# A macaron encoder layer on one core: unnormalised rows in the first gate products, 1/rms applied where they are resumed, twelve products begun ahead, norm weights loaded as rows

## The chip, the core and the metric

The kernel runs on one core of a Trainium2 chip. The metric is device microseconds of one execution; lower is better. Engines are named as the profile names them: PE (TensorE matmuls) with PEld (its weight loads), DVE (VectorE), ACT (ScalarE), POOL (GpSimd) and SP (SyncE, which issues most DMAs here; SPq is its queue).

## The reference, cut to what matters

```
x = x + 0.5 * swiglu(rms_norm(x, ffn1_norm), w_gate, w_up, w_down)     # first feed-forward
h = rms_norm(x, mix_norm); ... attention and mLSTM share one projection; x = x + merged @ w_out
x = x + 0.5 * swiglu(rms_norm(x, ffn2_norm), ...)                      # second feed-forward
return rms_norm(x, final_norm)

rms_norm(x, g) = x * rsqrt(mean(x*x) + eps) * g
swiglu(x, wg, wu, wd) = (silu(x @ wg) * (x @ wu)) @ wd
```

There are two sequences (`x_prompt`, `x_sample`) of 512 tokens with 1024 features; the feed-forwards have 2816 hidden features. All is float32. `rms_norm` multiplies each token (row of x) by one number, 1/rms, so `(x * g) @ w` can be taken first and each token's result multiplied by its 1/rms afterwards.

## The kernel before

**Precision.** A float32 operand is split into a high part (an ACT copy to fp32r, the format that TensorE multiplies) and a low part (DVE: source minus high). `product` (line 327) makes one 128x128 by 128x512 product of half the contraction: for each of four k it issues three matmuls (high·high, high·low, low·high), so 12 matmuls.

**Both sequences at once.** The 22 blocks (`NF`) of 128 hidden features are computed for both sequences together as a two-by-two block product with seven sub-products instead of eight (Strassen's scheme with Winograd's sums). The sums of operands are made by `right_sums` (line 281, for x) and `gu_left_b` (for weights). The seven operands are named `B11, B21, B22, T1, T2_, T3, T4`; two of them, `B11` and `B21`, hold only sequence 0 and only gate weights. Their product, `B11` plus `B21` in one PSUM bank, is the gate pre-activation of sequence 0.

**Begun ahead.** Because `B11` and `B21` need sequence 0 alone, `Up.begin` (line 438) computes them for the first `AHEAD` = 10 blocks while sequence 1 is still being loaded, turned, normed and summed: 24 matmuls each. The two results, `v1` (after `B11`) and `g0` (Silu of the whole), go to DRAM (`kept`). `Up.rest` then runs through all blocks in the order `ORDER`: a "resumed" block loads its pair (`resume`, two loads) and does five products, 60 matmuls; a "fresh" block does all seven, 84. Resumed and fresh alternate for eight pairs, then come four fresh and two resumed. In `gu_rest` (line 350) a fresh block's products are taken in the order B11, T2, B21, T1, T3, B22, T4, a resumed one's T2, T1, T3, B22, T4:

```
V_.tensor_tensor(u2, v1, Y, op=ALU.add)      # L364: needs v1 and product T2 in bank Y
product(Z, W[T1], xc[T1], True)
...
product(Y, W[T3], xc[T3], False)             # adds into the bank that L364 has read
```

So T3's first matmul waits for L364. `Sides.out` splits the results again and stores them (`rbuf`, a ring of seven SBUF rows, `ring.rows["o"]`) for the down projection.

**The start.** `load_x(0)` loads x_prompt in four blocks of 128 tokens; a first weight load, pinned behind the second block, and x_sample follow. As each block arrives, DVE and ACT sum its squares (`rows_rstd`, lines 1268 and 1270). PE turns the eight 128-feature groups (four 128x128 transposes each, L1251), ACT copies them out (`keep_x`, L1256), a chain of twelve small DVE operations makes 1/rms (`rsqrt_cols`, lines 162 to 192), four PE transposes broadcast it (L213), DVE multiplies every group by gain and 1/rms (L1275), and ACT and DVE split it (`put`, L278 and L279). Only then is a matmul of block 0 possible. The norm weights are loaded with the access `"(k p) -> p k"`, which takes one element at a time: 1024 elements of 4 bytes for `g1`, `gm` and `g2`, 512 for `hn`.

**Order.** A scheduler places instructions within each engine by priority; `pin` (`keep_in_program_order`) fixes a written order, `shifted(n)` changes a priority. Each engine and each DMA queue runs its list strictly in order.

## Time and profile before

| | |
|---|---|
| median of 3 runs | 2078.68 us (2077.52 to 2079.41) |
| the profiled execution: its time, its span | 2079.39 us, 2077.5 us |
| mean granted TensorE clock | 0.998 |
| busy: PE, PEld, DVE, ACT, POOL | 99%, 81%, 74%, 43%, 5% of the span |
| first products begun (B11, B21) until the first resumed block | 18.2 to 79.2 us |
| `Up.rest` of the first feed-forward | 79.2 to 446.9 us |

A row of the timeline gives start, duration (of the whole group where "xN" follows), engine, source line, operation, output<-input, shapes, and in brackets how long the engine had been idle and what ended that. Rows of one engine overlap by a few hundredths of a us, so the step between starts, not the duration, is what one instruction costs in a run of many. In a table of stretches each engine has its busy us and, in brackets, its instruction count; then come the granted TensorE clock, the DMA engines' busy share and GB/s.

### The profile page before, as it was taken

To read this page: it belongs to the slowest core of one execution; us is meant where nothing else is said; L and a number is where in the kernel's file an instruction comes from. 1 tells how busy PE (TensorE), PEld (TensorE's weight loads), DVE (VectorE), ACT (ScalarE), POOL (GpSimd) and SP (SyncE) were. 2 spreads that over 40 slices of the span, in tenths; PEclk is the share of its full clock that TensorE was granted. 3 is DMA by queue.
4 is the path that set the end of the run, shared out by engine and by line. 5 is a ranking of instruction groups with operands and counts; after the bars stand their busy time and mean duration, and the time that the engine had idled before them with its cause. 6 is when DMAs were issued, how large, how long until landed. Compare 5 with 4: busy or idle time off the path is not lost.

```text
span 2077.5 us, 27122 instructions
## 1 busy us (share of the span) xinstructions
PE 2059.7 (99%) x9451; PEld 1689.1 (81%) x9451; DVE 1547.5 (74%) x2798; ACT 901.6 (43%) x1653; POOL 103.7 (5%) x118
## 2 busy tenths in 40 slices
PE   8999999999999999999999999999999999999998
PEld 6888888888888877888877788888888888888887
DVE  7888888786797897575567645545888888796697
ACT  6544444442234566463344443323544444443224
POOL 1000000001003000100120000002000000000001
PEclk9999999999999999999999999999999999999999
DMA  9656555699766654777675245677656555599753
GB/s 280 206 171 195 193 172 183 197 338 365 267 218 239 219 159 170 260 240 271 218 270 176 102 152 183 204 255 239 210 168 220 176 190 182 166 346 350 267 204 125
DMA packets 307064, 454.31 MB, mean 219 GB/s; under 512 B 20064, under 2 KB 178864, under 8 KB 305904
## 3 DMA queue, kind: packets, MB, share of 16 engines
q1 hardware_dynamic: 304912, 446.87, 64.0%
q0 software_dynamic: 1872, 5.46, 0.8%
q8 instruction: 74, 1.21, 0.2%
q14 instruction: 62, 0.51, 0.1%
q10 hardware_dynamic: 144, 0.26, 0.0%
HBM read 285.63 MB, written 166.89 MB: 218 GB/s over the span
## 4 chain that ended last, share of the span: by engine, by line
PE 94%; DVE 2%; DMA 1%; ACT 1%; issue 0%; SPq 0%; ACTq 0%; DVEq 0%
PE mm L770 20%; PE pss L333 17%; PE pst L333 11%; PE mm L333 10%; PE mm L589 8%; PE pst L589 4%; PE pss L589 4%; PE mm L754 4%; PE pso L589 3%; PE pso L1044 1%; PE pss L1017 1%; PE pso L754 1%; PE pst L1036 1%; PE pso L1180 1%; PE pst L770 1%; PE pss L770 1%
## 5 line engine op out<-in xcount | busy, mean ns | idle before, releaser
L770 PE MATMUL mm<-xh,w 128*128 128x512 f32 x896 | 290.4, 394 | 0.0
L333 PE MATMUL pss<-xc,w 128*128 128x512 f32 x1056 | 256.3, 391 | 0.4 <-DVE t L364 0.4
L333 PE MATMUL mm<-xc,w 128*128 128x512 f32 x1056 | 253.1, 390 | 2.0 <-ACT w L291 1.0
L333 PE MATMUL pst<-xc,w 128*128 128x512 f32 x1056 | 253.8, 389 | 0.0
L333 PEld LDWEIGHTS pss<-xc,w 128*128 128x128 f32 x1056 | 196.9, 188 | 47.6 <-DVE t L364 7.0
L333 PEld LDWEIGHTS mm<-xc,w 128*128 128x128 f32 x1056 | 197.4, 188 | 44.8 <-ACT w L291 1.9
L333 PEld LDWEIGHTS pst<-xc,w 128*128 128x128 f32 x1056 | 198.1, 188 | 41.5 <-ACT t L368 0.4
L770 PEld LDWEIGHTS mm<-xh,w 128*128 128x128 f32 x896 | 167.7, 188 | 33.6
L589 PE MATMUL mm<-rt,w 128*128 128x512 f32 x765 | 178.8, 389 | 0.0
L770 PE MATMUL mm<-xl,w 128*128 128x512 f32 x448 | 176.3, 394 | 0.0
L589 PEld LDWEIGHTS mm<-rt,w 128*128 128x128 f32 x765 | 143.5, 188 | 29.8
L291 ACT ACTIVATE w<-t 128x512 fp32r<-128x512 f32 x176 | 106.9, 627 | 139.0 <-issue 55.2
L292 DVE TENSOR_TENSOR w<-t,w 128x512 fp32r<-128x512 f32 x176 | 118.1, 688 | 55.7 <-ACT w L291 53.8
L333 PE MATMUL pss<-xc,f 128*128 128x512 f32 x528 | 126.8, 389 | 0.0
L333 PEld LDWEIGHTS pss<-xc,f 128*128 128x128 f32 x528 | 99.1, 188 | 20.6
L672 ACT ACTIVATE w<-wr 128x512 fp32r<-128x512 f32 x72 | 45.1, 632 | 138.5 <-PE pso L589 65.2
L672 ACT ACTIVATE w<-t 128x512 fp32r<-128x512 f32 x82 | 51.8, 632 | 107.4 <-PE pst L589 62.4
L770 PEld LDWEIGHTS mm<-xl,w 128*128 128x128 f32 x448 | 84.3, 188 | 16.6
L589 PE MATMUL pss<-rt,w 128*128 128x512 f32 x396 | 93.7, 389 | 0.0
L589 PE MATMUL pst<-rt,w 128*128 128x512 f32 x396 | 93.7, 389 | 0.0
L239 ACT ACTIVATE w<-wr 128x1024 fp32r<-128x1024 f32 (+1 forms) x56 | 57.2, 1027 | 74.0 <-PE mm L770 30.3
L589 PEld LDWEIGHTS pst<-rt,w 128*128 128x128 f32 x396 | 74.3, 188 | 15.4
(359 smaller groups left out, 3653.6 us busy)
## 6 DMA issues: line engine op xcount, KB each, us to landing
rt<-rbuf SPq DMA_DIRECT2D x154, 512.0 KB, 5.5
wpark<-w SPq DMA_DIRECT2D x104, 512.0 KB, 3.4
w<-wpark SPq DMA_DIRECT2D x104, 512.0 KB, 4.6
wr<-in_ffn_w_gate_dram SPq DMA_DIRECT2D x62, 512.0 KB, 5.3
rbuf<-tab SPq DMA_DIRECT2D x102, 256.0 KB, 4.0
wr<-in_ffn_w_up_dram SPq DMA_DIRECT2D x44, 512.0 KB, 4.6
rbuf<-f SPq DMA_DIRECT2D x72, 256.0 KB, 4.0
wr<-in_w_in_dram SPq DMA_DIRECT2D x36, 512.0 KB, 6.0
```

The costliest lines, as they stand in the source:

```text
L239: pin(nc.scalar.activation(hi, raw, AF.Copy))
L291: pin(nc.scalar.activation(t[:, 0], src, AF.Copy))
L292: pin(V_.tensor_tensor(t[:, 1], src, f(t[:, 0]), op=ALU.subtract))
L333: nc.tensor.matmul(p, a[:, k, :], xt[:, b, k, :], start=(first and k == 0 and i == 0), stop=(k == HK_ - 1 and i == 2), skip_group_check=True)
L589: nc.tensor.matmul(p, u[:, a, d * P:(d + 1) * P], r[:, b, ts], start=(first and q == 0 and k == 0), stop=(q == len(us) - 1 and k == 2), sk ...
L672: nc.scalar.activation(hi, src, AF.Copy)
L754: nc.tensor.matmul(p[b][:, :N], a[:, k, bs], w_[:, kl, :], start=(k == 0 and i == 0), stop=(k == KD - 1 and i == 2))
L770: nc.tensor.matmul(p, a[:, k, :], b, start=(k == 0 and i == 0), stop=(k == n - 1 and i == 2))
L1017: nc.tensor.matmul(p, qT[:, h, b * P:(b + 1) * P], kv[:, hk * 2 + j, :], start=(j == 0), stop=(j == 1))
L1036: nc.tensor.transpose(p[:, b * P:(b + 1) * P], Ps[b][:, kb * P:(kb + 1) * P], ident)
L1044: nc.tensor.matmul(po, Vst[:, kv_, hk, :], w, start=(kv_ == 0 and i == 0), stop=(kv_ == 3 and i == 1))
L1180: nc.tensor.matmul(po, vm[:, a, t, hs_], b, start=(t == 0 and n == 0), stop=(t == 3 and n == 2))
```

## The change

It has four parts.

1. The start. x_prompt's rows are turned and split without 1/rms: `first_x` takes each turned group from PSUM, ACT writes gain times x as the high part, DVE the rest as the low part. Six of the eight groups hold their banks while the four token blocks arrive, each block turned as it lands; two matmuls of ones (`busy(2)`) are placed between blocks. The first weight load stands directly behind x_prompt, in two halves, and is split in two halves too. 1/rms of sequence 0 is worked out after that and kept as a row table, `R0`. The float32 copies of x0 are multiplied by gain and `R0` later, in the loop that makes the sums.
2. Where they are resumed. `begin` stores the unscaled products (`Copy` in place of `Silu`). `scale_first` multiplies `v1` and `g0` by `R0` on POOL and applies Silu on ACT: for resumed blocks after their loads, for fresh blocks after the copies out of PSUM. `R0` takes one of the seven rows of ring "o" in the first feed-forward. In that feed-forward POOL gets 44 multiplications of 128x512, and ACT 22 more Silus.
3. `AHEAD` is 12, in both feed-forwards. `ORDER` becomes ten pairs of resumed and fresh and two resumed.
4. The four norm weights are loaded as 8 (or 4) rows of 128 elements and turned on PE; the load of the gate bias moves to the start.

In the changed program POOL's list in a pair reads: resumed block's `g0`, its `v1`, the fresh block's `v1`, its `g0`. DVE's list around the pair is otherwise as before (L364 is L378 there).

```diff
-    def gu_left_a(rg, pin=lambda i: i):
+    def gu_left_a(rg, lo=None, pin=None, between=None):
         wa = w8_tile()
-        w_pair(wa, rg.rearrange("p (a k) c -> p a k c", a=2), pin)
+        rv = rg.rearrange("p (a k) c -> p a k c", a=2)
+        if between:
+            for a in range(2):
+                w_pair(wa[:, :, a], rv[:, a], lo, pin)
+                between()
+        else:
+            w_pair(wa, rv, lo, pin or (lambda i: i))
...
+    def scale_first(row, v1, g0):
+        if v1 is not None:
+            G_.tensor_tensor(v1, v1, row, op=ALU.mult)
+        if g0 is not None:
+            G_.tensor_tensor(g0, g0, row, op=ALU.mult)
+            nc.scalar.activation(g0, g0, AF.Silu)
...
             X = gu_first_a(W, xc, v1)
+            if row is not None:
+                scale_first(row, v1, None)
             second()
-            gu_first_b(X, W, xc, g0)
+            gu_first_b(X, W, xc, g0, AF.Silu if row is None else AF.Copy)
+            if row is not None:
+                scale_first(row, None, g0)
...
-    AHEAD = 10
+    AHEAD = 12
...
             self.ring.rows["o"] += tables(FFN_ROWS)
+            if row:
+                self.row = self.ring.rows["o"].pop()
...
                 for t, d in zip(got, self.kept.pop(j)):
                     nc.sync.dma_start(t, d)
+                if self.row is not None:
+                    scale_first(self.row, *got)
...
+    for t, src, row, q in gains:
+        q.dma_start(row, src.rearrange("(k p) -> k p", p=P))
...
     load_x(0)
-    raw0 = up.fetch(0, (0,), raws[0][:, 1, 0:1])
-    load_x(1)
-    raw1 = [up.fetch(j, (0,))[0] for j in (1, 2)]
+    for a in range(2):
+        nc.sync.dma_start(half(raw0, a), half(up.v[0], a)[:, :, 0:P])
+    raw1 = up.fetch(1, (0,))
+    load_x(1)
+    raw1 += up.fetch(2, (0,))
+    busy(8)
...
+    for b in range(4):
+        for k, p in enumerate(banks):
+            pin(turn(0, k, b, p))
+        if b < 3:
+            busy(2)
+            squares(0, b, sq, (V_, nc.scalar), pin)
...
     def first_x(k):
-        scaled(x0[k], x0r[k], k, R0)
-        put(xc[B11 if k < HK_ else B21], k % HK_, x0[k])
+        t, kk, p, g = xc[B11 if k < HK_ else B21], k % HK_, banks[k], g1[:, k:k + 1]
+        pin(nc.scalar.activation(t[:, 0, kk, :], p, AF.Copy, scale=g))
+        pin(V_.scalar_tensor_tensor(t[:, 1, kk, :], p, g, f(t[:, 0, kk, :]), op0=ALU.mult, op1=ALU.subtract))
...
+    ahead()
+    W = [gu_left_a(raw0, None, pin, ahead)]
+    late_turn(PT)
+    ahead()
+    keep_x(0, 0, banks[0], x0[0])
+    late_turn(PS)
+    W.append(gu_left_a(raw1[0], None, pin))
+    for k in todo:
+        first_x(k)
+    for k in range(1, 4):
+        keep_x(0, k, banks[k], x0[k])
+    squares(0, 3, sq, (V_, nc.scalar), pin)
+    rs = rows_rstd(sq)
...
+        for t, kk in ((x0[k], k), (x0[k + HK_], k + HK_)):
+            scaled(t, t, kk, R0)
-        for j in ((3,), (4, 5), (6, 7), (8, 9))[k]:
+        for j in ((3, 4), (5, 6), (7, 8, 9), (10, 11))[k]:
             up.begin(j, up.left(j))
```

The last edit is made in the second feed-forward's loop too.

145 lines of the change are left out of this document (84 added, 61 removed).

## The prediction

> **What bounds the kernel now.** I read the busy shares first, then the stretches of the start, the timelines of PE, DVE and ACT there, and last one pair of blocks of `Up.rest`. From the page and from the table of stretches:
>
> ```profile
> PE 2059.7 (99%) x9451; PEld 1689.1 (81%) x9451; DVE 1547.5 (74%) x2798; ACT 901.6 (43%) x1653; POOL 103.7 (5%) x118
> ```
>
> ```profile
> 2.00:4.00 2.00, 2.00 (x12) 2.00 (x11) 0.00 (x0) 0.21 (x2) 0.86 (x3) 1.00 0.93 336
> 4.00:6.00 2.00, 1.07 (x6) 0.69 (x5) 0.93 (x3) 0.96 (x3) 0.27 (x2) 1.00 0.93 334
> 6.00:8.00 2.00, 0.04 (x1) 0.00 (x0) 0.47 (x2) 0.48 (x2) 1.99 (x3) 0.95 0.99 176
> 8.00:10.00 2.00, 0.60 (x2) 0.31 (x3) 0.78 (x3) 0.82 (x3) 0.96 (x2) 0.50 1.01 397
> 100.00:300.00 200.00, 200.00 (x876) 163.69 (x876) 169.85 (x266) 86.67 (x146) 0.00 (x0) 1.00 0.60 193
> ```
>
> PE is the bound: from 100 to 300 us it has no idle time, so only two things can move the total: what PE waits for at the start, and what the change adds to PE's waits later. The start, on PE's timeline:
>
> ```profile
> 18.18 0.50 PE L333 MATMUL mm<-xc,w 128*128 128x512 f32 x1 [0.54 <-ACT xc L278]
> ...
> 22.71 11.21 PE L333 MATMUL mm<-xc,w 128*128 128x512 f32 x48 [0.27 <-DVE w L292]
> ...
> 41.53 11.52 PE L333 MATMUL mm<-xc,w 128*128 128x512 f32 x48
> ...
> 64.67 0.60 PE L1251 MATMUL pss<-ident,raw 128*128 128x128 f32 x4
> 65.11 0.60 PE L1251 MATMUL pst<-ident,raw 128*128 128x128 f32 x4
> ...
> 79.17 1.07 PE L333 MATMUL pss<-xc,w 128*128 128x512 f32 x4
> ```
>
> The first real matmul comes at 18.18, a dense run at 22.71, and at 79.17 the first resumed block begins, after 10 x 24 = 240 matmuls. A transpose costs 0.44 / 4 = 0.11 us (64.67 to 65.11). The steady price of a matmul is in one pair of blocks:
>
> ```profile
> 249.70 0.39 PE L333 MATMUL mm<-xc,w 128*128 128x512 f32 x1
> ...
> 260.86 2.88 PE L333 MATMUL pss<-xc,w 128*128 128x512 f32 x12
> 263.58 2.88 PE L333 MATMUL mm<-xc,w 128*128 128x512 f32 x12
> ...
> 269.02 2.88 PE L333 MATMUL pss<-xc,w 128*128 128x512 f32 x12
> ...
> 282.62 0.39 PE L333 MATMUL mm<-xc,w 128*128 128x512 f32 x1
> 282.98 1.21 PE L333 MATMUL pss<-xc,w 128*128 128x512 f32 x4
> ```
>
> From 260.86 to 263.58 twelve take 2.72, 0.2267 each. 240 of them are 54.4 us: of the 79.17 some 23 us are start, not work.
>
> **The change, part 1: when x_prompt is there.** T is the landing of its last block.
>
> ```profile
> raw<-in_x_prompt_dram SPq DMA_DIRECT2D x4, 512.0 KB, 5.6
> ...
> g<-in_ffn_norm_dram POOLq DMA_DIRECT2D x1, 4.0 KB, 7.4
> ```
>
> ```profile
> 9.92 0.69 DVE L1268 SCALAR_TENSOR_TENSOR R<-raw 128x512 f32<-128x512 f32 x1 [0.73 <-DMA raw<-in_x_prompt_dram]
> ...
> 10.92 0.17 DVE L162 TENSOR_SCALAR rs<-cs 128x4 f32<-128x4 f32 x1
> ...
> 13.11 0.16 DVE L192 SCALAR_TENSOR_TENSOR rs<-rs,rs 128x4 f32<-128x4 f32 x1
> 15.20 1.41 DVE L1275 SCALAR_TENSOR_TENSOR t<-f,g,pst 128x512 f32<-128x512 f32 x2 [1.93 <-ACT t L1256]
> 16.52 1.22 DVE L292 TENSOR_TENSOR w<-wr,w 128x1024 fp32r<-128x1024 f32 x1
> ...
> 18.31 1.89 DVE L279 TENSOR_TENSOR xc<-t,xc 128x512 fp32r<-128x512 f32 x3
> ```
>
> T is 9.9 now. The 4 KB of `g1` take 7.4 us to land, one element at a time, and in 6 to 8 us the DMA engines are 0.99 busy but move 176 GB/s, against 334 before. That load becomes eight rows, and the three like it go as well. With 334 in that stretch the same bytes are through (334 - 176) x 2 / 397 = 0.8 us earlier, at 9.1; if nothing behind x_prompt overtook it, its 2.1 MB less the 1.34 moved by 6.0 would need 2.1 us more, 8.1. I take 8.5; the ends are 8.1 and 9.9 (no gain).
>
> **Part 1: from T to the dense run.** Now 1/rms (12 operations, 2.35 us from 10.92), its broadcast, the scaling and the split all lie between T and the first matmul. In the changed program the broadcast comes after 35 matmuls. After T the first group has its last transpose and its high half by about T + 1.0 (0.4 of transposes and 0.6 of ACT). Then DVE paces: eight low halves at 0.67 (15.20, two in 1.41), two half splits of weights at 0.60 (18.31, three in 1.89), one full split at 1.22, together 7.8, until T + 8.8. ACT has the same number of shorter steps and is ahead. PE does the B11 half of block 0 and eleven matmuls of its B21 half as the groups come, and ends with these at about T + 9.0; behind them stand block 1's twelve with all operands ready, 2.7 us, to T + 11.7. Then PE waits for the broadcast: DVE's last square (0.69), its read and sum (0.3) and the chain (2.35) end at T + 12.1, four transposes and one matmul at T + 12.8. That is 36 matmuls at 21.3. What remains: 288 - 36 = 252 matmuls, 57.1 us; 38 transposes, 4.2 us; and small waits, for which I take 0.7 (now, from 41.53 on, 156 matmuls and 16 transposes need 37.1 of 37.6). The first resumed block then begins at 83.3. The kernel of before would have 48 more matmuls done at 79.17 + 10.9 = 90.05. **The start saves 6.7 us** (7.1 at T = 8.1, 5.3 at 9.9).
>
> The clock falls to 0.50 after PE had 0.04 us of work in 6 to 8 us. In the new start transposes and the matmuls of ones fill most of each gap between blocks, so I price this at nothing; at half clock block 1's twelve would take 2.7 us more. The first weights, 0.5 MB directly behind x_prompt, are wanted at T + 0.95; at 397 GB/s the first half lands by T + 0.7. If late, all shifts by as much, 1 us at most.
>
> **Part 2: two more blocks ahead.** Matmuls are the same in number. A pair costs 282.62 - 249.70 = 32.92 us for 144 x 0.2267 = 32.64: 0.28 is lost where T3 of the resumed block waits for L364 (below). Ten pairs instead of eight lose 0.56 more in each feed-forward, **1.1 us**. The extra stores and loads go to DMA engines that are 0.60 busy (100 to 300): nothing.
>
> **Part 3: scaling on POOL.** 44 multiplications, in the pairs four each. DVE, ACT and SP in the pair above:
>
> ```profile
> 263.87 0.68 DVE L364 TENSOR_TENSOR t<-t,pss 128x512 f32<-128x512 f32 x1
> ...
> 267.65 1.30 DVE L292 TENSOR_TENSOR w<-t,w 128x512 fp32r<-128x512 f32 x2 [1.72 <-ACT w L291]
> ...
> 270.80 1.23 DVE L292 TENSOR_TENSOR w<-wr,w 128x1024 fp32r<-128x1024 f32 x1 [1.13 <-ACT w L291]
> ...
> 274.66 0.69 DVE L377 TENSOR_TENSOR t<-t,pst 128x512 f32<-128x512 f32 x1 [1.31 <-PE pst L333]
> ...
> 282.25 0.68 DVE L364 TENSOR_TENSOR t<-t,pss 128x512 f32<-128x512 f32 x1
> ```
>
> ```profile
> 266.50 0.60 ACT L348 ACTIVATE t<-mm 128x512 f32<-128x512 f32 x1 [3.16 <-PE mm L333]
> ```
>
> ```profile
> 259.76 0.80 SPq L467 DMA_DIRECT2D t<-kept  x2
> ```
>
> ```profile
> t<-kept SPq DMA_DIRECT2D x17, 256.0 KB, 2.9
> ```
>
> What such a POOL operation costs, and costs DVE, is seen in the down projection:
>
> ```profile
> 614.39 1.30 POOL L156 TENSOR_TENSOR R<-R,f 128x512 f32<-128x512 f32 x1 [115.47 <-ACT f L155]
> ```
>
> ```profile
> 614.17 0.68 DVE L622 SCALAR_TENSOR_TENSOR xs<-mm,xs 128x512 f32<-128x512 f32 x1
> 614.77 1.48 DVE L611 TENSOR_TENSOR xs<-xs,e 128x512 f32<-128x512 f32 x1
> ```
>
> POOL runs until 615.69. DVE's L622, fed from PSUM, takes its usual 0.68; L611, with both inputs in SBUF, lasts until 616.25, so it did its 0.6 of work after POOL had ended. The Trainium skill states this as a rule (SBUF — State Buffer, "Who interferes with whom"): a DVE instruction with two SBUF inputs and a GpSimd instruction that reads SBUF exclude each other for the whole instruction. By that rule most of DVE's work in a pair stands still during each POOL operation; the trace agrees.
>
> The pair under this exclusion: the kept loads, issued at 259.76 and 260.2, land 2.9 later, 262.7 and 263.1. POOL lets DVE's running operation end (0.6), scales `g0` until 264.5, lets one more pass, scales `v1` until 266.4, then the fresh block's `v1` until 267.7. L364, at 263.87 now, waits for that and ends at 268.4; PE wants it at 269.02, when T3 starts. Queued behind the waiting L364 are L397, L314, three L292, L316, L372 and L374, 5.5 us, and 0.6 more since the fresh `g0` (copied out at 266.50) holds them up: done at 274.4. L377 cannot start before 274.66 anyway. So DVE's idle 1.72 + 1.13 + 1.31 = 4.16 us hides it all, with 0.6 and 0.25 us to spare. I take 0.1 a pair, **1.0 us**; the ends are nothing and, with all four operations stopping DVE for 1.30, 5.2 - 4.16 = 1.04 a pair. The place matters because from 274.66 DVE has no gap until L364 of the resumed block at 282.25, which ends at 282.93, and PE's T3 starts at 282.98: there, each delay of DVE is PE's. ACT's 22 added Silus stand behind POOL in its list, but ACT is 43% busy in 100 to 300 (86.67 of 200) and idles 3.16 before 266.50: nothing.
>
> **Part 4, with one answer.** Six rows instead of seven in ring "o", 11 uses per 32.9 us, come back after 18 us on average; three small transposes and copies of the norm weights lie in the sum above. Nothing in the second feed-forward beside part 2.
>
> **Sum.** 6.7 - 1.1 - 1.0 = 4.6 us saved. The profiled execution took 2079.39 (1.9 around its span of 2077.5) and would take 2074.8; against the median, 2078.68, it is 2074.1. About 0.2%, 4.2 us, is what a measurement of this kernel can tell from no change.
>
> **Rivals.**
> - *POOL stops DVE for longer than DVE's idle time.* Place: the ten pairs. It decides from 4.16 us of blocking a pair, or from kept loads landing 0.6 us later than I have them. At the full 1.04 a pair it costs 10.4, not 1.0: 2078.68 - 6.7 + 1.1 + 10.4 = 2083.5, slower. For it: the exclusion is seen in the row above, and DVE is 85% busy. Against it: PSUM-fed operations pass, and POOL works partly while DVE waits. This is also what the skill's rule gives without those two reliefs.
> - *The start gains less and the pairs lose some.* x_prompt lands at 9.9 as now (5.3 saved) and each pair loses 0.4: 5.3 - 1.1 - 4.0 = 0.2 saved, 2078.5, no change. For it: x_prompt's own bytes at full speed fill most of the time to 9.9. Against: the stretch at 176 GB/s.
> - *The pairs lose nothing, not even the 0.28 for the added ones, and T is 8.1:* 7.1 saved, 2071.6. Against: L364's edge at 282.93 stands as before.
>
> **Chances.** Forecast 0.50, first rival 0.16, second 0.26, third 0.08. The forecast's own range is 2072.5 to 2076.5; about a sixth of it falls within 0.2%. So faster by over 0.2%: 0.42 + 0.08 = 0.50; within 0.2%: 0.26 + 0.08 = 0.34; slower 0.16. The range takes in the second rival and most of the first: 2071.0 to 2082.5.
>
> **What would show it.** Right: x_prompt's last block before 9.1; the first 128x512 matmul near 10; the first resumed block near 83; pairs of 32.9 to 33.0 us; POOL's multiplications at 1.3 to 1.9 us. Wrong: a first resumed block later than 86, pairs above 33.3, or PE waits for L378 (the old L364) in fresh blocks.

## The result and the profile after

The changed kernel is slower: 2086.43 us (median, 2084.45 to 2088.69) against 2078.94 us for the kernel before in the same runs (2077.52 to 2079.79), a ratio of 1.0037 [1.0024, 1.005], 7.5 us more. Predicted were 2074.1 us, range 2071.0 to 2082.5. The profiled execution took 2086.04 us with a span of 2084.1; that of the kernel before had a span of 2077.5.

The line of busy shares on the page of the changed kernel:

```profile
PE 2064.5 (99%) x9467; PEld 1691.1 (81%) x9467; DVE 1584.6 (76%) x2802; ACT 916.4 (44%) x1678; POOL 169.8 (8%) x159
```

PE is still the bound. Where its time went is on its timeline (changed kernel; L1268 are the turns of x_prompt, L210 the broadcast of 1/rms, L336 the real matmuls, L608 the down projection):

```profile
10.35 0.44 PE L1268 MATMUL pss<-ident,raw 128*128 128x128 f32 x2 [1.67 <-DMA raw<-in_x_prompt_dram]
...
11.98 3.37 PE L336 MATMUL mm<-xc,w 128*128 128x512 f32 x7 [0.31 <-ACT w L288]
...
23.65 0.65 PE L210 MATMUL pst<-ident,rs 128*128 128x128 f32 x4
24.06 5.96 PE L336 MATMUL mm<-xc,w 128*128 128x512 f32 x25
...
31.93 0.73 PE L336 MATMUL mm<-xc,w 128*128 128x512 f32 x2 [1.28 <-ACT f L344]
...
89.23 2.88 PE L336 MATMUL pss<-xc,w 128*128 128x512 f32 x12
...
98.99 5.49 PE L336 MATMUL pss<-xc,w 128*128 128x512 f32 x12 [4.16 <-DVE t L378]
104.28 3.00 PE L336 MATMUL pst<-xc,w 128*128 128x512 f32 x12
...
112.56 2.88 PE L336 MATMUL pss<-xc,w 128*128 128x512 f32 x12
...
431.42 3.01 PE L336 MATMUL pss<-xc,w 128*128 128x512 f32 x12 [0.45 <-DVE t L378]
...
448.09 3.01 PE L336 MATMUL pst<-xc,w 128*128 128x512 f32 x12 [0.29 <-ACT t L382]
...
453.69 6.28 PE L608 MATMUL mm<-rt,w 128*128 128x512 f32 x27
```

Three things are read from it. First, the first real matmul comes at 11.98, 6.2 us earlier than before (18.18), yet the first resumed block begins at 89.23. The mark for this is the kernel before with twelve blocks ahead (e7 below; its timeline of PE):

```profile
89.70 2.88 PE L333 MATMUL pss<-xc,w 128*128 128x512 f32 x12
...
446.78 6.28 PE L589 MATMUL mm<-rt,w 128*128 128x512 f32 x27
```

Of 6.7 us that the start was to save, 0.5 are left. Second, in the first resumed block PE waits 4.16 us for L378, and the twelve matmuls after that take 104.28 - 98.99 = 5.29 us, not 2.72; the granted clock is 0.50 there:

```profile
98.00:102.00 4.00, 3.01 (x7) 2.43 (x8) 3.83 (x7) 2.04 (x4) 0.00 (x0) 0.50 0.07 14
```

(Table of stretches, changed kernel; the clock is the 0.50.) From the first resumed block to the next fresh block's T2 are 112.56 - 89.23 = 23.33 us; before it was 17.04 (79.17 to 96.21): 6.3 lost in one place. Third, the pairs after it repeat every 32.92 us (112.56, 145.48, 178.39, 211.31), the same as before, up to the last two resumed blocks, which stand next to each other: from the first fresh T2 to the down projection it is 453.69 - 112.56 = 341.13 us, and 340.07 in e7 (106.70 to 446.78), so 1.1 are lost there, most of it in the waits at 431.42 and 448.09. The down projection begins 453.69 - 446.86 = 6.8 us late and nearly all of the 7.5 is there.

Who held L378 in that block (timelines of POOL, ACT and DVE, changed kernel):

```profile
87.79 3.94 POOL L357 TENSOR_TENSOR t<-t,tab 128x512 f32<-128x512 f32 x1 [37.82 <-DMA t<-kept]
```

```profile
91.76 0.63 ACT L358 ACTIVATE t<-t 128x512 f32<-128x512 f32 x1 [3.53 <-POOL t L357]
...
92.77 1.05 ACT L288 ACTIVATE w<-wr 128x1024 fp32r<-128x1024 f32 x1
```

```profile
89.89 0.68 DVE L323 TENSOR_TENSOR t<-wr,t 128x512 f32<-128x512 f32 x1
...
93.86 1.23 DVE L289 TENSOR_TENSOR w<-wr,w 128x1024 fp32r<-128x1024 f32 x1 [3.28 <-ACT w L288]
...
98.26 0.68 DVE L378 TENSOR_TENSOR t<-t,pss 128x512 f32<-128x512 f32 x1
```

The resumed `g0` lands at 87.79, and POOL's multiplication of it takes 3.94 us, until 91.73. DVE works without a gap until 90.57 (L323 is its last operation there), so POOL ends 1.16 us after DVE has stopped; its next multiplication, from 91.7 on beside an idle DVE, takes 1.30. ACT's Silu of `g0` (L358) waits 3.53 us for the first; queued behind it on ACT are the high halves of the fresh block's weights (L288); DVE waits 3.28 us for those, and L378 stands behind the low halves in DVE's list. PE needs L378 for T3.

In the start PE waits twice for the copy out of PSUM (L344). A wait like the 0.69 us at 17.84 is in every run that starts this way, with six rows too (e9, 0.69). The 1.28 at 31.93 goes back to a store. Timelines of ACT and of SP's queue, changed kernel:

```profile
31.28 0.60 ACT L344 ACTIVATE f<-mm 128x512 f32<-128x512 f32 x1 [1.91 <-DMA kept<-f]
```

```profile
19.68 5.84 SPq L1277 DMA_DIRECT2D xbuf<-t  x7
...
25.61 0.62 SPq L462 DMA_DIRECT2D kept<-f  x1
```

`begin` copies its results into a ring of two SBUF rows, which come free when the stores to `kept` have landed; these stand behind seven stores of x, and the DMA engines are full then:

```profile
20.00:25.00 5.00, 4.86 (x24) 3.72 (x23) 3.61 (x16) 4.78 (x10) 0.00 (x0) 1.00 1.11 373
25.00:30.00 5.00, 5.00 (x23) 3.84 (x22) 2.95 (x5) 4.38 (x14) 0.00 (x0) 1.00 0.96 356
```

### The profile page after: what moved, and what is told of

Its sections match the earlier page's. It is cut to its first block, busy times and chain, and to the rows that moved or that the text cites. A ratio compares the mean times of both kernels' runs of the same rounds, so it can differ in the third digit from the quotient of the medians.

```text
span 2084.1 us, 27262 instructions
## 1 busy us (share of the span) xinstructions
PE 2064.5 (99%) x9467; PEld 1691.1 (81%) x9467; DVE 1584.6 (76%) x2802; ACT 916.4 (44%) x1678; POOL 169.8 (8%) x159
## 4 chain that ended last, share of the span: by engine, by line
PE 92%; DVE 3%; DMA 3%; ACT 1%; issue 1%; POOL 0%; SPq 0%; ACTq 0%; POOLq 0%
PE mm L781 20%; PE pss L336 16%; PE pst L336 11%; PE mm L336 9%; PE mm L608 8%; PE pst L608 4%; PE pss L608 4%; PE mm L765 4%; PE pso L608 3%; PE pso L1055 1%; PE pss L1028 1%; PE pso L765 1%; PE pst L1047 1%; PE pso L1191 1%; PE pst L781 1%; PE pss L781 1%
## 5 line engine op out<-in xcount | busy, mean ns | idle before, releaser
L336 PE MATMUL pss<-xc,w 128*128 128x512 f32 x1056 | 259.3, 395 | 4.6 <-DVE t L378 4.6
L336 PE MATMUL mm<-xc,w 128*128 128x512 f32 x1056 | 255.2, 393 | 2.8 <-ACT f L344 2.0
L336 PE MATMUL pst<-xc,w 128*128 128x512 f32 x1056 | 253.9, 389 | 0.3 <-ACT t L382 0.3
L336 PEld LDWEIGHTS pss<-xc,w 128*128 128x128 f32 x1056 | 198.2, 189 | 53.7 <-DVE t L378 12.8
L336 PEld LDWEIGHTS mm<-xc,w 128*128 128x128 f32 x1056 | 197.4, 188 | 45.4 <-ACT f L344 2.6
L336 PEld LDWEIGHTS pst<-xc,w 128*128 128x128 f32 x1056 | 198.3, 188 | 42.0 <-ACT t L382 0.7
L608 PE MATMUL mm<-rt,w 128*128 128x512 f32 x765 | 178.8, 389 | 0.0
L288 ACT ACTIVATE w<-t 128x512 fp32r<-128x512 f32 x176 | 106.1, 627 | 150.2 <-issue 70.9
L608 PEld LDWEIGHTS mm<-rt,w 128*128 128x128 f32 x765 | 143.5, 188 | 29.8
L289 DVE TENSOR_TENSOR w<-t,w 128x512 fp32r<-128x512 f32 x176 | 127.8, 746 | 26.3 <-ACT w L288 25.3
L336 PE MATMUL pss<-xc,f 128*128 128x512 f32 x528 | 126.8, 389 | 0.0
L336 PEld LDWEIGHTS pss<-xc,f 128*128 128x128 f32 x528 | 99.1, 188 | 20.6
L608 PE MATMUL pss<-rt,w 128*128 128x512 f32 x396 | 93.7, 389 | 0.0
L608 PE MATMUL pst<-rt,w 128*128 128x512 f32 x396 | 93.7, 389 | 0.0
L608 PEld LDWEIGHTS pst<-rt,w 128*128 128x128 f32 x396 | 74.3, 188 | 15.4
```

The lines of the kernel that those rows point to most:

```text
L288: pin(nc.scalar.activation(t[:, 0], src, AF.Copy))
L289: pin((lo or V_).tensor_tensor(t[:, 1], src, f(t[:, 0]), op=ALU.subtract))
L336: nc.tensor.matmul(p, a[:, k, :], xt[:, b, k, :], start=(first and k == 0 and i == 0), stop=(k == HK_ - 1 and i == 2), skip_group_check=True)
L608: nc.tensor.matmul(p, u[:, a, d * P:(d + 1) * P], r[:, b, ts], start=(first and q == 0 and k == 0), stop=(q == len(us) - 1 and k == 2), sk ...
```

## The experiments

Two theories on the 4.2 us stall and the tail: A, ACT's Silu queued behind POOL holds up the weights' splits of the first resumed block; B, POOL's multiplications cost DVE, and so PE, something in every pair (the prediction's first rival). On the start: small loads delay x_prompt, and stores delay the ring of two rows. Each kernel was timed beside the kernel before, and the ratio is to that one's median (2078.94 to 2080.29 us). "Resumed" is where PE begins the first resumed block, "down" where the down projection begins, in us.

| kernel | first matmul | resumed | down | median us | ratio [95%] |
|---|---|---|---|---|---|
| before | 18.18 | 79.17 | 446.86 | 2078.94 | |
| after | 11.98 | 89.23 | 453.69 | 2086.43 | 1.0037 [1.0024, 1.005] |
| e1: Silu late | 12.10 | 88.93 | 448.30 | 2081.14 | 1.0009 [1.0, 1.0018] |
| e2: no scaling | 11.89 | 87.55 | 446.02 | 2079.64 | 1.0002 [0.9993, 1.0011] |
| e3: ten ahead | 12.02 | 82.91 | 452.11 | 2085.48 | 1.0029 [1.0018, 1.004] |
| e4: small loads late | 10.98 | 89.09 | 451.62 | 2085.63 | 1.0029 [1.0018, 1.0041] |
| e5: x stored by POOL | 12.04 | 91.91 | 457.19 | 2089.16 | 1.004 [1.0026, 1.0053] |
| e6: e1 + e4 + e5 | 10.10 | 92.68 | 453.57 | 2084.79 | 1.0023 [1.0014, 1.0032] |
| e7: before, twelve ahead | 17.21 | 89.70 | 446.78 | 2081.05 | 1.0005 [0.9996, 1.0014] |
| e8: e6, ten ahead | 10.81 | 84.16 | 452.65 | 2085.16 | 1.0023 [1.0014, 1.0031] |
| e9: six rows | 11.94 | 88.65 | 453.92 | 2084.52 | 1.0027 [1.0017, 1.0037] |
| e10: e9 + e1 | 11.88 | 89.50 | 450.48 | 2081.14 | 1.0009 [1.0001, 1.0018] |
| e11: e10 + e4 | 10.60 | 89.59 | 450.39 | 2082.32 | 1.0012 [1.0003, 1.0021] |
| e12: norms as columns later | 10.19 | 87.82 | 454.03 | 2086.68 | 1.0035 [1.0021, 1.0049] |
| e13: e10 + scaling held | 12.15 | 86.22 | 446.48 | 2079.21 | 0.9999 [0.9991, 1.0008] |
| e14: all start edits | 10.07 | 83.58 | 446.87 | 2079.04 | 0.9998 [0.9989, 1.0007] |
| e15: e14, loads at the last block | 10.29 | 83.86 | 445.83 | 2078.83 | 0.9991 [0.9983, 1.0] |
| e16: e15, Silu late at the end | 10.92 | 84.30 | 442.95 | 2079.55 | 0.9998 [0.9989, 1.0007] |
| e17: e15, loads near 60 us | 10.34 | 83.96 | 443.43 | 2076.47 | 0.9984 [0.9975, 0.9993] |

The positions come from the one profiled execution of each kernel. It lies within 1.4 us of the median, but for e6, e9, e10 and e16, where it took 1.6, 2.0, 1.6 and 3.5 us longer. From the down projection to the end are 1630.2 to 1631.4 us in all of them (before: 1630.6), so their differences arise ahead of it; only e16 has 1638.2.

### The first resumed block: e1, e2, e3

e1 loads the first two resumed blocks' `g0`, and queues its scaling and Silu, only behind `u2` (L378's output):

```diff
             V_.tensor_tensor(u2, v1, Y, op=ALU.add)
+        if late_g0:
+            t, d = late_g0.pop()
+            G_.tensor_copy(t[:, 0:1], u2[:, 0:1])
+            nc.sync.dma_start(t, d)
+            scale_first(row, None, t)
...
+                if self.row is not None and j < 2:
+                    scale_first(self.row, got[0], None)
+                    late_g0.append((got[1], d1))
+                    return got
```

> The changed kernel, but the gate product g0 of the first two resumed blocks is loaded (and so scaled and put through Silu) only once that block's L378 has run, so that ACT's list no longer stands at that Silu before the weight splits. Theory A (the loss is made at the first resumed block: ACT waits there 3.5 us for POOL and a load, DVE for ACT, PE 4.2 us for DVE, and then runs at half clock): 6 us less than the changed kernel, about 2080, and no PE wait for L378 near 99 us. Theory B (POOL keeps DVE out over all ten pairs): nothing changes, 2086.

Measured 2081.14 us, 5.3 less than the changed kernel. PE at T3 of the first resumed block (timeline, e1):

```profile
94.88 3.02 PE L336 MATMUL pss<-xc,w 128*128 128x512 f32 x12 [0.35 <-DVE t L380]
```

The wait of 4.16 is 0.35 and the twelve take 3.02 us. The next fresh T2 comes 16.97 us after the resumed block's begin, as before. Theory A holds.

e2 leaves out the 44 multiplications by 1/rms; all else stays, the Silus too:

```diff
     def scale_first(row, v1, g0):
         if v1 is not None:
-            G_.tensor_tensor(v1, v1, row, op=ALU.mult)
+            pass
         if g0 is not None:
-            G_.tensor_tensor(g0, g0, row, op=ALU.mult)
             nc.scalar.activation(g0, g0, AF.Silu)
```

> The changed kernel with the 44 multiplications on POOL left out (1/rms is not applied to the gate products of the first sequence; their Silu stays). Theory A: the wait at the first resumed block shrinks by the two POOL operations before its Silu (5.2 us there), but ACT still waits for the load: 3 to 6 us less, 2080 to 2083, and the other pairs stay at 32.9 us. Theory B: each pair gets shorter too; all in all 6 to 10 us less.

Measured 2079.64. Without POOL the stall is 1.05 us (timeline, e2):

```profile
94.20 3.02 PE L336 MATMUL pss<-xc,w 128*128 128x512 f32 x12 [1.05 <-DVE t L377]
```

What is left of the wait is not POOL's; e1, which also takes the load and the Silu out of this place, leaves 0.35. After the first resumed block, from the first fresh T2 to the down projection, e2 needs 340.80 us, the changed kernel 341.13 and e1 342.40. All the multiplications outside that block are thus worth 0.3 to 1.6 us, and the pairs repeat every 32.9 us in all three. Theory B, 1 us in each pair, falls; the little that is left lies mostly at the end (e1 waits 0.46 and 0.71 us in the last two resumed blocks, e2 0.87).

e3 is the changed kernel with `AHEAD = 10` and the loops to match.

> The changed kernel with ten blocks begun ahead instead of twelve, in both feed-forwards. If the two more pairs cost 0.28 us each in both: 1.1 us less, 2085.3. If the ten-block order also brings the first resumed block closer to the loop's DVE work, its wait grows: up to 4 us more, 2090. Theory A and B both leave the rest as it is.

Measured 2085.48, 1 us below the changed kernel (the intervals overlap), and the stall stays in another form: PE waits 3.52 us for a weight split when the first resumed block begins (timeline, e3). Two more blocks ahead are not the cause of the loss.

```profile
82.91 4.62 PE L336 MATMUL pss<-xc,w 128*128 128x512 f32 x12 [3.52 <-ACT w L288]
```

### The start, one edit at a time: e4, e5, e6, e8, e7

e4 puts the small loads (three norm weights, gate bias) behind the landing of x_prompt:

```diff
     load_x(0)
+    small_loads()
...
+    def small_loads():
+        for t, src, row, q in gains[1:]:
+            n = row.shape[0]
+            nc.gpsimd.tensor_copy(row[:, 0:1], raws[0][0:n, 3, 0:1])
+            q.dma_start(row, src.rearrange("(k p) -> k p", p=P))
+        nc.gpsimd.tensor_copy(gbias[:, 0:1], raws[0][:, 3, 0:1])
...
```

(The one-column copies make each load wait for x_prompt's last block.)

> The changed kernel with the four small loads on POOL's queue (three norm weights as rows, the gate bias) held back until the last block of x_prompt is there. If these loads are what holds x_prompt's last block (DMA moves 74 to 212 GB/s from 7.5 to 9.5 us): that block lands at 8.3 to 9.0 instead of 10.35, and the total falls by 1 to 1.5 us, to 2085. Rival: the 0.5 MB and 0.5 MB of weights and x_sample behind x_prompt are what delays it: the block stays at 10.3 and the total at 2086.4.

Measured 2085.63. The stretch of 8 to 10 us, changed kernel and then e4:

```profile
8.00:10.00 2.00, 0.68 (x7) 0.49 (x4) 0.00 (x0) 0.00 (x0) 0.00 (x0) 1.00 0.79 167
```

```profile
8.00:10.00 2.00, 1.98 (x18) 1.78 (x17) 0.70 (x2) 1.01 (x3) 0.64 (x5) 1.00 1.15 316
```

With the small loads gone the DMA engines move 316 GB/s in place of 167 and the last block is turned at 9.35, 1.0 us earlier. Which of the four loads it is, the issues and landings of the changed kernel tell (POOL's timeline, then DMA issues with their us to landing):

```profile
2.89 0.52 POOL L1260 DMA_DIRECT2D tab<-in_mlstm_head_norm_dram  x1
3.40 0.58 POOL L1261 DMA_DIRECT2D gbias<-in_mlstm_gate_bias_dram  x1
```

```profile
tab<-in_mlstm_head_norm_dram POOLq DMA_DIRECT2D x1, 2.0 KB, 4.9
gbias<-in_mlstm_gate_bias_dram POOLq DMA_DIRECT2D x1, 8.0 KB, 7.0
```

The last of the rows has landed at 2.9 + 4.9 = 7.8 us. In 8 to 10 us only the gate bias is still under way; it lands at 10.4, with x_prompt's last block. No run moves the gate bias alone.

In e4 the slow stretch has moved along with the loads (issued at 9.84 to 11.61). Its stretch of 15 to 17 us, where the changed kernel moves 405 GB/s:

```profile
15.00:17.00 2.00, 1.22 (x6) 0.65 (x5) 2.00 (x3) 2.00 (x5) 0.00 (x0) 1.00 0.97 207
```

The 1.0 us is lost again by 31 us, where PE waits 2.13 for L344 in place of 1.28 (timeline, e4):

```profile
31.22 0.73 PE L336 MATMUL mm<-xc,w 128*128 128x512 f32 x2 [2.13 <-ACT f L344]
```

e5 issues sequence 0's stores of x on POOL's queue, so that the `kept` stores are not queued behind them on SP:

```diff
-        nc.sync.dma_start(xbuf[s][:, k, :], xt)
+        (nc.sync if s else nc.gpsimd).dma_start(xbuf[s][:, k, :], xt)
```

> Edit: the changed kernel with the stores of the first sequence's raw x rows issued on POOL's queue in place of SyncE's; nothing else. In the changed kernel ACT's copy of v1 waits 1.9 us for its row of the two-row ring, PE waits 0.7 and 1.3 us for these copies (L344) and runs at about half clock from 32 to 36 us, and the first resumed block begins at 89.2 us. Theory C (the start's gain is lost because the store that frees a kept row stands behind the seven stores of x rows in SyncE's queue): PE's waits for L344 fall below 0.5 us in all, the first resumed block begins at 85 to 87 us, the time is 2 to 3 us below the changed kernel's 2086.4, so 2083 to 2085 (the stall inside the first resumed block stays). Theory D (the start is as long as the work and the granted clock make it, wherever the stores are queued): the first resumed block begins at 88.7 to 89.5 us, whatever PE waits for, and the time stays at 2086.

Measured 2089.16, slower still, which no theory had. ACT waits longer for a `kept` store (timeline, e5), and PE runs at 0.50 from 34 to 38:

```profile
27.52 0.60 ACT L351 ACTIVATE f<-mm 128x512 f32<-128x512 f32 x1 [3.39 <-DMA kept<-f]
```

So taking x's stores out of SP's queue does not free the ring sooner. The DMA engines are as full as before (1.10 and 0.95 busy in 20 to 25 and 25 to 30 us), and the `kept` stores issued in 15 to 30 us take 6.1 us to land, 5.5 in the changed kernel. Whether stores are slower on POOL's queue in themselves wasn't tried. e6 and e8 put e1, e4 and e5 together, with twelve and with ten ahead:

> Edit: the changed kernel with three edits together: the g0 halves of the first two resumed blocks are loaded and put through Silu only once u2 is made; the three norm rows for later stages and the gate bias are loaded only when x_prompt's last block has landed; the stores of the first sequence's x rows go out on POOL's queue. The first alone gave 2081.1, the second alone 2085.6 (its 1 us was given back at the wait for the copy of v1). Theory C: with the wait for the copy of v1 gone the early landing is kept, the first resumed block begins at 84 to 86 us and the time is 2076 to 2079, so below the 2079.6 of the kernel before. Theory D: the first resumed block begins at 88 to 89 us and the time is that of the first edit alone, 2080.5 to 2081.5.

> Edit: the kernel of the three edits together with ten blocks begun ahead in place of twelve. In the changed kernel itself ten in place of twelve moved 2086.4 to 2085.5, with the stall then at the first resumed block's weights (3.5 us for ACT's split). Theory A (the stall is ACT's queue, which POOL holds up): with the Silu late that wait is gone here too, and the time is within 1 us of the three edits with twelve. Rival (with ten, the weights of the first resumed block are late on their own, for DMA or for DVE): PE still waits 2 us or more at the first resumed block and the time is 1.5 to 3 us above the three edits with twelve.

Measured 2084.79 and 2085.16. In e6 the last block is turned so early that everything comes to the ring at once (timeline, e6):

```profile
32.18 0.81 PE L336 MATMUL mm<-xc,w 128*128 128x512 f32 x2 [3.94 <-ACT f L344]
```

In e8 PE waits 5.35 us for L344 near 34 us; the weight wait of e3 is down to 0.5, so the late Silu, the one of the three edits that bears on it, removed that one too. e7 is the kernel before with `AHEAD = 12` and nothing else:

> Edit: the kernel before with twelve blocks begun ahead in both feed-forwards in place of ten, and nothing else of the change (norm applied first, as before). It measures the part of the change that the prediction priced at 0.28 us for each of two more pairs in each of two feed-forwards, 1.1 us. Prediction's step: 2080.2 to 2081.2, the period of a pair stays at 32.9 us. Rival: the two extra blocks are begun where PE stood idle before in the start, so the time is 2079.6 or up to 1 us lower; they would also meet the two-row ring of kept halves, and then PE waits more than 1 us for L344's line in this kernel too and the time is above 2081.5.

Measured 2081.05, 1.2 us above the kernel before in its job, with an interval that takes in nothing and 2.9 us: in line with the estimate of 1.1 for two more pairs, not a proof of it. Its profiled execution reaches the down projection at 446.78, the kernel before at 446.86, so in the first feed-forward no loss is seen. Its resumed block at 89.70 is the mark for the starts below (the prediction worked out 90.05).

### The ring and what stands behind it: e9 to e13

e9 gives the first three blocks six rows, x_prompt's tile that has been read, in place of two:

```diff
+    spare = up.ring.rows["k"]
+    up.ring.rows["k"] = [raws[0][:, b, i * S:(i + 1) * S] for b in range(3) for i in range(2)]
     up.begin(0, W[0])
...
     up.begin(2, W[2])
+    up.ring.rows["k"], up.ring.at["k"] = spare, 0
```

> Edit: the changed kernel with six rows in place of two for the kept halves of the first three blocks; the six are the part of x_prompt's raw tile that has been read by then; nothing else. In the run with the x stores on POOL's queue ACT's copy waited longer (3.4 us in place of 1.9) for its row: the row's store was out at 24.5 us and its landing took 3 us more, while the 16 DMA engines were taken over 90% of the time until 27 us. Theory E (the start's gain is lost because a store of a kept half, in a stage in which the DMA engines are full, holds its row, so ACT's copy, so the PSUM bank, so PE): with six rows PE's waits for L344's line fall from 2.0 us to below 0.8 in all, no half clock between 32 and 36 us, and the first resumed block begins at 85.5 to 87.5 us in place of 89.2; the time is 2083 to 2085, as the stall inside the first resumed block (4.2 us and the clock behind it) stays. Theory D (the start is as long as the loads and stores make it: x_sample, the weights and the stores of x have to pass before 30 us whatever PE does): PE waits as long for weights or for x_sample's rows, the first resumed block begins at 88.5 to 89.5 us and the time stays at 2086.

Measured 2084.52. The wait for L344 near 31 us is gone, and 0.6 us of the start is gained in the profiled execution, not the 1.3 that it lasted: PE now waits 1.1 us for the copies of the turned norm weights. The first resumed block still stalls 4.18 us. e10 adds e1's edit, e11 also e4's:

> Edit: the changed kernel with the six rows for kept halves and with the g0 halves of the first two resumed blocks loaded and put through Silu only once u2 is made. The latter alone gave 2081.1. Theory E: 2 to 3.5 us less than that, 2077.5 to 2079, so at or just below the kernel before's 2079.7. Theory D: 2080.5 to 2081.5.

> Edit: as the run before it, and the three norm rows for later stages and the gate bias are loaded only when x_prompt's last block has landed. Alone this brought x_prompt's last block 1.0 us earlier and gave the 1.0 us back at the wait for L344's copy. Theory E: with that wait gone 1 us is kept, 2076.5 to 2078 us, the first resumed block begins at 84.5 to 86.5 us. Theory D: no more than the run before it, 2080.5 to 2081.5, or PE waits for weights where it waited for x_prompt.

Measured 2081.14 and 2082.32. e1's gain is there; the start gains nothing (89.50, 89.59). Timelines of PE and DVE in e10 say why:

```profile
32.44 0.22 PE L1377 MATMUL pst<-ident,tab 8*128 8x8 f32 x1 [1.98 <-DVE gain L1381]
```

```profile
28.25 4.06 DVE L1314 SCALAR_TENSOR_TENSOR t<-t,g,tab 128x512 f32<-128x512 f32 x6 [2.43 <-DMA xbuf<-t]
```

DVE multiplies the copies of x0 in place (L1314) and must wait until their stores have been read out, 28.25 us; 4.06 us of such work then stand ahead of the norm copies and weight splits that PE is waiting for, and the clock falls to 0.50 from 34 to 36. In e11 the same place shows the half clock, and the weights of block 4 arrive late (timeline of ACT, e11):

```profile
32.78 1.06 ACT L288 ACTIVATE w<-wr 128x1024 fp32r<-128x1024 f32 x1 [1.74 <-DMA wr<-in_ffn_w_gate_dram]
```

e12 takes the three later norm weights and the gate bias out of the start altogether (loaded as columns behind the sixteenth block of `Up.rest`, counted 15 in the code; no turns and copies on PE and DVE):

```diff
-    for t, src, row, q in gains:
+    for t, src, row, q in gains[:1]:
...
-        nc.tensor.transpose(pg[:, i * KD:i * KD + n], row, ident[0:n, 0:n])
...
+    def mix_gains():
+        for t, src, _, _ in gains[1:]:
+            pin(nc.gpsimd.dma_start(t, src.rearrange("(k p) -> p k", p=P)))
...
+    tail = up.rest(raw0, 15, mix_gains)
```

> Edit: the changed kernel with the three norm weights of later stages and the gate bias loaded during the resumed blocks, the norm weights straight as columns, as the kernel before lays them out; so no row loads, no transposes and no copies for them in the start; ffn1_norm stays a row. Theory F (part 4 of the change costs in the start: it slows x_prompt's last block and its transposes stand in PE's queue at 30 us): x_prompt's last block lands at 8.5 to 9.3 us in place of 10.35, but the wait for L344's copy and the stall in the first resumed block stay, so no more than 1 us of it shows: 2085 to 2086.5. Rival (part 4 costs nothing beyond the landing, and the landing is kept): 2084.5 to 2085.

Measured 2086.68, no better than the changed kernel, though the last block is turned at 8.57 (timeline, e12):

```profile
8.57 0.44 PE L1267 MATMUL pss<-ident,raw 128*128 128x128 f32 x2
```

A landing 1.8 us earlier gives 1.4 us at the resumed block, where the stall is still there (3.2 us), and near 31 us PE waits 2.69 for L344. At 352.73 PE waits 2.02 us more; e14 shows that wait. e13 is e10 with the in-place scalings of x0 pinned behind the blocks begun and behind the first scaling of sequence 1:

```diff
-            scaled(t, t, kk, R0)
+            pin(scaled(t, t, kk, R0))        # moved behind up.begin of the same k
```

> Edit: six rows and late Silu as in the run that gave 2081.1, and VectorE's in-place scalings of x0 held until after the first scaling of the other sequence, so that they no longer stand, waiting for the stores of x, ahead of the norm copies and the fourth and fifth blocks' splits. Theory F (VectorE's order): PE's wait for the norm copies near 30 us (2.0 us in that run) and the half clock behind it go, the first resumed block begins at 84 to 86.5 us in place of 89, the time is 2077 to 2079. Theory D (the transfers set it: the fifth block's weights land at 33 us whatever the order): PE waits for weights from 31 to 34 us instead, the first resumed block begins at 88 us or later and the time is 2080 to 2081.5.

Measured 2079.21; the resumed block begins at 86.22, 3.3 us earlier than in e10, and the wait for the norm copies is gone.

### All covers off, and what comes after: e14 to e17

e14 is e13 with e12's loads, block 0's up weights fetched behind blocks 3 to 6, and the weight splits of blocks 3 and 4 ahead of the squares:

```diff
+            with shifted(-40 if k < 1 else 0):
+                Wj = up.left(j)
+            up.begin(j, Wj)
+        if k == 1:
+            raw0 = [raw0] + up.fetch(0, (1,))
```

> Edit: as the second run, and also the norm weights of later stages and the gate bias loaded later (as in the first run), the up weights of block 0 (needed only at the first fresh or resumed block) loaded behind those of blocks 3 to 6, and the split of block 3's weights put ahead of part of the squares of x_sample. It takes away every wait of PE seen in the start so far, and moves 0.5 MB out of the stage before 30 us. Theory F or D alike: PE runs from 11 us on with waits below 2 us in all, the first resumed block begins at 82.5 to 85 us, and the time is 2075 to 2077.5, below the kernel before's 2079.7. If a further wait stands behind these, it is named by PE's list of waits and the time is 2078 to 2080.

Measured 2079.04. The first resumed block begins at 83.58; the prediction had 83.3. But the four small loads have moved to where POOL scales (timelines of POOL, ACT and PE, e14):

```profile
333.94 1.09 POOL L1407 DMA_DIRECT2D gain<-in_mix_norm_dram  x1
```

```profile
344.53 0.63 ACT L358 ACTIVATE t<-t 128x512 f32<-128x512 f32 x1 [4.23 <-POOL t L357]
```

```profile
345.70 4.61 PE L336 MATMUL pst<-xc,w 128*128 128x512 f32 x12 [2.02 <-ACT t L389]
```

The same chain as in the first resumed block: POOL late, ACT behind it, PE behind ACT, then half clock. e15 moves the loads to the last block, e16 also queues the last two resumed blocks' Silus late, e17 has them in the start's loop near 60 us, held by a copy that reads the other sequence's data:

```diff
-    tail = up.rest(raw0, 15, mix_gains)
+    tail = up.rest(raw0, NF - 1, mix_gains)                                # e15
...
-                if self.row is not None and j < 2:
+                if self.row is not None and (j < 2 or j >= AHEAD - LAST):   # e16, with e15's line
...
+        if k == 2:                                                         # e17, in place of mix_gains
+            for c, src, _, _ in gains[1:]:
+                G_.tensor_copy(c[:, 0:1], x1u[:, 0:1])
+                nc.gpsimd.dma_start(c, src.rearrange("(k p) -> p k", p=P))
...
```

> Edit: as the run with all start edits, but the norm columns and the gate bias are loaded behind the last block in place of within the resumed blocks (POOL multiplies no kept halves after that). If the 2.0 us wait at 345.7 us and the half clock behind it come from POOL's loads standing ahead of the row multiplications: both go, about 4 us, the down projection begins at 442.5 to 443.5 us and the time is 2074.5 to 2076. Rival (the resumed blocks lose as much elsewhere, as DVE is busier while POOL multiplies): the wait goes, others of together 2 us or more take its place, and the time is 2077.5 to 2079.

> Edit: as the run before it, and the late Silu also for the last two resumed blocks, which stand next to each other (PE waited 0.45 us for u2 there). If that wait too comes from a Silu queued on ACT ahead of work that is due: 0.4 to 0.5 us less than the run before it. Rival: the late load makes g0 itself late, T4 waits, and it is 0.3 to 1 us more.

> Edit: as the run with all start edits and the loads last, but the norm columns and the gate bias are loaded near 60 us, behind x1's scaled rows of the third step, where POOL has nothing else. If the 2.4 us wait at 440 us came from the place of these loads: it goes, the down projection begins at 442.5 to 443.8 us and the time is 2075 to 2077. Rival (the down projection's first weights are late whenever the phase ends early): a wait of 1.5 us or more for the same copy or for the down weights stays, the down projection begins at 445 to 447 us and the time stays at 2078 to 2079.

e15: 2078.83, without the wait at 345.70 but with a new one at the end of the blocks (timelines of PE and ACT, e15), where an ACT split in the down projection's weights waits 5.41 us for its DMA and a product waits behind it:

```profile
440.22 3.06 PE L336 MATMUL pst<-xc,w 128*128 128x512 f32 x12 [2.42 <-ACT t L389]
```

```profile
439.05 0.63 ACT L703 ACTIVATE w<-wr 128x512 fp32r<-128x512 f32 x1 [5.41 <-DMA wr<-in_ffn_w_down_dram]
```

e16: 2079.55. The 0.46 us that it aimed at, PE's wait for L380 at 421.37 in e15, is gone, but PE now waits 4.0 us in the down projection for the split of L703. So the 442.95 in the table is no gain, and the 0.7 us more than e15 is the rival's size without the rival's wait for T4. The profiled execution is the one 3.5 us above the median. e17: 2076.47 against 2079.75 for the kernel before, ratio 0.9984 [0.9975, 0.9993], 3.3 us below it and 10 below the changed kernel. Its stretch of 8 to 10 us and PE's timeline:

```profile
8.00:10.00 2.00, 2.00 (x19) 1.79 (x17) 0.20 (x1) 0.92 (x2) 0.00 (x0) 1.00 1.16 322
```

```profile
10.34 2.49 PE L336 MATMUL mm<-xc,w 128*128 128x512 f32 x7 [0.31 <-ACT w L288]
...
83.96 2.88 PE L336 MATMUL pss<-xc,w 128*128 128x512 f32 x12
...
90.54 3.01 PE L336 MATMUL pss<-xc,w 128*128 128x512 f32 x12 [0.98 <-DVE t L380]
...
443.43 6.28 PE L620 MATMUL mm<-rt,w 128*128 128x512 f32 x27
```

The start is 89.70 - 83.96 = 5.7 us ahead of the kernel before with twelve blocks. By the down projection 446.78 - 443.43 = 3.4 are left: 0.98 went in the wait above and 1.2 in PE's other waits for the same L380 and for L389 in later resumed blocks.

## Why the prediction was wrong, step by step

- **"I take 8.5; the ends are 8.1 and 9.9" (T).** The last block was turned at 10.35, 1.85 late and outside both ends. The prediction took the slow stretch (176 GB/s in 6 to 8) to end with the element-wise load. It moved: 167 GB/s in 8 to 10, with the gate bias, which the change itself brings to the start, still under way; the rows had landed by 7.8. Without these loads the turn comes at 9.35 (e4) and 8.57 (e12), close to 8.5. By the landing times the rows did what they were to do, and what failed is that the added load, the gate bias, was not priced.
- **"36 matmuls at 21.3", T + 12.8.** Nearly right: 35 at 23.65, T + 13.3, when the broadcast begins, and 36 at about 24.3 (24.06 and one matmul), T + 13.9, so 1.1 too long. The clock, 0.56 in 12 to 14 us, is 0.5 of it: e1 had 1.00 there, and its broadcast begins at T + 12.8 (last block turned at 10.47; timeline, e1):

```profile
23.25 0.65 PE L210 MATMUL pst<-ident,rs 128*128 128x128 f32 x4
```

  The price of nothing for the clock was thus good to half a microsecond here, but not later: after the waits of 4.16 us and, in e14, of 2.02 us twelve matmuls took 5.29 and 4.61.
- **"small waits, for which I take 0.7", so the first resumed block at 83.3.** The step that failed in the start. After the 36 matmuls it took 89.23 - 24.3 = 64.9 us, not 83.3 - 21.3 = 62.0. With the 1.85 and the 1.1 above, that makes the 5.9 us by which the resumed block is late against 83.3. The 0.7 came from a stretch of the old start in which block after block finds its inputs landed. In the new start work reaches the ring, DVE and the DMA engines 6 us sooner while these finish when they did, so covers lie one behind the other: x_prompt's landing, two rows waiting for their stores, in-place scalings waiting for x's stores, norm turns, block 4's weights. Taking off one gave half or all of it to the next (e4, e9 to e11), and what e12 kept at the resumed block was gone by the down projection, with its loads in a new place; with five off (e14, e17) the resumed block begins at 83.58 and 83.96. The sum of PE's work was right; the covers were not priced.
- **"The extra stores and loads go to DMA engines that are 0.60 busy (100 to 300): nothing."** For the extra stores, which go out after 80 us, nothing contradicts it. What it left out is the stores of the first blocks, which now go out between 20 and 30 us, where the engines are 0.96 to 1.11 busy.
- **"ACT's 22 added Silus stand behind POOL in its list … nothing."** The step that failed in the blocks, 6.3 us. ACT's 43% is a mean; at the first resumed block ACT's next work is what DVE and then PE need, and POOL took 3.94 us there, not 1.30. The place was named and priced by a busy share instead of by what is queued behind the waiting instruction. e1 moves this Silu, with its load and multiplication, and takes back 5.3. In the pairs the same Silus left the step at 32.92.
- **POOL's blocking, 1.0.** The size came out, the place did not, so that is luck. In the pairs it was too much: their step stayed at 32.92. But the last two resumed blocks, which the prediction did not look at, lost 1.1 (341.13 against 340.07 in e7), and leaving out POOL's multiplications takes back only 0.3 of it (e2). In the pairs DVE was slowed, from 688 to 814 ns for a low half of weights (groups of instructions by form, kernel before and then changed kernel, 100 to 430 us), and its idle time covered that, as argued:

```profile
L292 DVE TENSOR_TENSOR w<-t,w 128x512 fp32r<-128x512 f32 x78 | 52.3, 688 | 26.0 <-ACT w L291 25.2
```

```profile
L289 DVE TENSOR_TENSOR w<-t,w 128x512 fp32r<-128x512 f32 x82 | 65.2, 814 | 0.7
...
L355 POOL TENSOR_TENSOR t<-t,tab 128x512 f32<-128x512 f32 x20 | 34.3, 1734 | 19.8 <-DMA t<-kept 19.8
L357 POOL TENSOR_TENSOR t<-t,tab 128x512 f32<-128x512 f32 x19 | 27.6, 1454 | 242.1 <-DMA t<-kept 229.7 <-ACT t L351 12.5
```

- **Two more pairs, 1.1.** Measured 1.2 (e7) with an interval that takes in nothing, and nothing is seen of it in the profiled executions: e7 reaches the down projection 0.1 us ahead of the kernel before, and from there to the end the changed kernel, with the two pairs in its second feed-forward, needs 1630.4 us, the kernel before 1630.6. It stays open.
- **The sum.** Predicted 4.6 saved, measured 7.5 lost (6.6 between the two profiled spans), some 12 apart. 6.2 of it is the start (0.5 saved instead of 6.7) and 6.3 the first resumed block. The other terms hardly count: 1.1 lost in the last two resumed blocks stands where 1.0 was taken for the pairs, and the 1.1 for two more pairs is not seen in the profiles. Against e7 the first feed-forward loses 6.3 + 1.1 - 0.5 = 6.9 us, which is the late down projection.
- **The rivals.** The first, POOL stopping DVE, came near the time (2083.5) by another mechanism: not 1.04 us in each of ten pairs, but once, through ACT. In the first resumed block POOL's 3.94 us is the rule that the prediction quoted (the Trainium skill, SBUF — State Buffer, "Who interferes with whom") seen from its other side: while DVE runs operations with two SBUF inputs, POOL is the one that waits. The trace agrees, 3.94 us against 1.30. The prediction let POOL have its turn after DVE's running operation (0.6); here it ended only 1.16 us after DVE's last one, 2.8 us on. It had asked only what POOL costs DVE.
- **What would show it.** "The first resumed block later than 86" and "PE waits for L378" were the named signs of error and both appeared, the wait in the first resumed block rather than in fresh ones.

## What to carry to other kernels

A start that is made shorter is worth what the next cover allows: list what else finishes at a fixed time (stores that free a ring, small loads, in-place work behind a store) and price the start by the latest of them, since taking off one alone brought the first resumed block 0.1 to 1.4 us forward here (e4, e9, e12) and all of them 5.3 (e17). An operation put on an idle engine is not free if another engine's list waits for it: ask what stands directly behind the waiting instruction at the one place where no slack has been built up yet, the first iteration, and queue it after the work that PE needs next. When a small load is moved, its new place has neighbours too (e12, e14, e15).

## What the runs showed of the hardware

- A wait on PE could cost nearly twice its length: after 4.16 us the granted clock was 0.50 and twelve matmuls took 5.29 us in place of 2.72, after 2.02 (e14, and e12 likewise) 4.61. After 0.35, 1.05 and, in e15, 2.42 us they took 3.02 to 3.06, so the length of the wait alone does not decide it; what does wasn't tried.
- While the gate bias (8 KB) on POOL's queue was under way, the DMA engines moved 167 GB/s in 8 to 10 us (changed kernel), against 316 and 322 without it (e4, e17); moved to a later place, it and the last rows went with 207 GB/s in 15 to 17 us (e4), against 405. That the gate bias is the cause is read from the landing times.
- POOL's 128x512 multiplication lasts 1.30 us beside an idle DVE, 1.45 to 1.73 on average in the pairs, and 3.94 where DVE had no gap for the first 2.8 us of it.
- x's stores on POOL's queue did not bring the `kept` stores forward while the DMA engines were full (e5: 6.1 us to landing in place of 5.5, and ACT's longest wait for one 3.39 us in place of 1.91).
